# Where the first fp16 part of the attention weights is made, and the model of times behind an engine order

## The chip, the cores and the metric

The kernel runs on one core of a Trainium2 chip. The metric is the device time of one execution in microseconds; the median of several executions counts. A core has five engines that run side by side and meet at semaphores: TensorE (PE in the profile, its weight loads PEld), VectorE (DVE), ScalarE (ACT), GpSimd (POOL), and SyncE (SP), whose queue issues every DMA of this kernel.

## The reference

One decoder layer on x of 512 tokens by 1024 channels, float32, with two attention mixers in parallel:

```python
h = rms_norm(x, norm_w)
proj = h @ w_in                      # q, k, v of both mixers, gates z_a, z_b, gate_b, gate_m
o_a = moba_mixer(...)                # 8 heads of 64
o_b = nsa_mixer(...)                 # 8 heads in 2 groups: compressed, selected and window branch
y_a = o_a * silu(z_a); y_b = o_b * silu(z_b)
g_m = sigmoid(gate_m)
merged = g_m[..., :D] * (y_a @ w_branch_a) + g_m[..., D:] * (y_b @ w_branch_b)
out = x + merged @ w_out
# in each attention unit, for causal keys:
logits = q @ k.T * scale + bias_tab[t5_bucket(dist)]
p = softmax(where(dist >= 0, logits, -1e30)); o = p @ v
```

At 512 tokens every block of the block-sparse mixers is among the selected ones, so the selected and window branches and mixer A are causal softmax attention with a relative bias. There are 24 such units: 8 heads of mixer A, and 8 heads of mixer B with two branches each.

## The kernel before

**Products.** Large products are made in split precision: each float32 operand is a high part (rounded to TensorE's format) and a low remainder, and three matmuls are summed (`mm3`, L418). The high part of a weight tile is made by ScalarE or GpSimd (L386 to L388, L362 to L364), the low part by VectorE or GpSimd as a subtraction (L390, L366). Projections with tokens as rows are `gemm_tok` (PSUM tiles `pgt`), those with channels as rows `gemm_chan` (`pgc`), the branch products `branch` (`pbr`), and the last one `products` (`po`).

**Attention units.** A `Unit` handles one head and branch in four query blocks b of 128, with L = 128 (b + 1) keys. For each block: two matmuls give the scores in PSUM (`sps`, L1044, L1045); VectorE adds the bias, leaves the result in the SBUF tile `sb` and takes the extreme of each row (L1065); ScalarE takes the exponential and its sum (L1076) and multiplies the sum by the gate (L1078); VectorE takes the reciprocal (L1079). P is then kept as two fp16 tiles: GpSimd writes the first part, the exponential times the reciprocal (L1080), and VectorE the remainder (L1081). `send` issues one DMA transpose of both parts (`dma_transpose`, L230) into the tile `dst`, which frees `sb` when it has landed; `pv` multiplies the transposed parts by V (L1094, PSUM tile `O`), and `o_out` (L1121, L1125) takes the result out. There are 6 `sb` buffers, 2 score buffers, 1 `O` and 2 `dst`.

**What sets the order.** The program switches the automatic scheduler off and writes each engine's order by itself. While the program is built, a planner in Python plays the work through: `Chain` objects hold the steps of one piece of work, each step with a dictionary of costs in ns by engine ("A" ScalarE, "D" or "d" VectorE, "P" or "p" GpSimd). `step` gives the step to the engine on which it would end first; the small letters "d" and "P" also mark steps that keep VectorE and GpSimd from working at the same time (`lock`, in `ends`). A step's result is put `OUT[engine] + LAT` ns after its end. Streams of TensorE work (`Run`: scores, values, products, preparation) are generators; the main loop takes the next one that is ready by a margin, and by its share. `dma` and `dma_transpose` issue a transfer on SP at the planner's current time and return when it should have landed; `free["Q"]` is the time at which the transfer engines are free. So every cost in the planner can change the order on all five engines, and the engine of a step with a choice. The chip then runs that fixed order, each engine waiting at its semaphores.

The costs by which a step with a choice is placed:

```python
def cd(n):    return 65 + 1.045 * n
def cg(n):    return 180 + 2.08 * n
def either(n):    return {"d": cd(n), "P": cg(n)}
```

Of the kernel before, what the change touches and what calls it, by code (L numbers as in the profile page):

```python
# [15 lines left out]
AF = mybir.ActivationFunctionType  # L16
ALU = mybir.AluOpType
AX = mybir.AxisListType

S = 512  # L20
D = 1024
DH = 64
P = 128
# [33 lines left out]
MARGIN = 300  # L57
XQ = 1200
XW = 1700.0
# [39 lines left out]
def hybrid_kernel(ctx: ExitStack, tc: tile.TileContext, x, x0, xT, wtok, wchan, gains, w1,  # L99
                  relone, wbr, wout, consts, out):  # L100
    nc = tc.nc
# [18 lines left out]

    now = [0.0]
    heap, seq = [], itertools.count()
    free = {"A": 1900.0, "D": 0.0, "P": 800.0, "Q": 400.0}
    OUT = {"A": 105, "D": 85, "P": 30}
    done = {}
    ap_ = ctx.enter_context(tc.tile_pool(name="att", bufs=NATT))
# [9 lines left out]
    def ca(n):  # L136
        return 93 + 0.834 * n
# [4 lines left out]
    def cd(n):  # L142
        return 65 + 1.045 * n

    def cg(n):
        return 180 + 2.08 * n
# [4 lines left out]
    def either(n):  # L151
        return {"d": cd(n), "P": cg(n)}
# [10 lines left out]
    class Chain:  # L163


        def __init__(c, t=None, held=False):
            c.t = now[0] if t is None else t
            c.q = deque()
            c.held = held
# [49 lines left out]
        def ready(c):  # L219
            return None if c.q else c.t  # L220

    def dma(dst, src, n, t=None):

        nc.sync.dma_start(out=dst, in_=src)
        free["Q"] = max(free["Q"], (now[0] if t is None else t) + 1000) + max(450, n * P / 360)
        return free["Q"] + 1000

    def dma_transpose(dst, src, blocks):

        nc.sync.dma_start_transpose(out=dst, in_=src)  # L230
        free["Q"] = max(free["Q"], now[0] + 1000) + blocks * 120
        return free["Q"] + 1300

    def run_until(t):
        now[0] = max(now[0], t)
# [85 lines left out]
    class Stream:  # L321
# [47 lines left out]
        def split(w, upto):  # L369
            for i in range(w.next, min(upto, len(w.tiles))):  # L370
                w.next = i + 1
                if isinstance(w.tiles[i], Sum):
                    if i not in w.chain:
                        w.split_sum(i)
                    continue
                while i not in w.raw:
                    w.load()
                w.ahead -= 1
                n, *squares = w.tiles[i][1:]
                (raw, t), hi, lo = w.raw.pop(i), w.mk_hi()[:, :n], w.mk_lo()[:, :n]  # L380
                w.out[i] = hi, lo
                c = w.chain[i] = Chain(max(now[0], t))

                def f(e, hi=hi, raw=raw):
                    if e is nc.scalar:
                        e.copy(hi, raw)  # L386
                    else:
                        e.tensor_scalar(hi, raw, 1.0, 1.0, op0=ALU.mult, op1=ALU.mult)  # L388
                c.do({"A": ca(n), "P": 78 + n}, f).mark((w, 0, i))
                c.do(either(n), lambda e, hi=hi, lo=lo, raw=raw: e.tensor_sub(lo, raw, hi.bitcast(F32))).mark((w, 1, i))  # L390
                for o, m, g, acc, fn in squares:
                    c.do({"A": 190 + 0.834 * m}, lambda e, z=raw[:, o:o + m], g=g, acc=acc: e.activation(
                        z, z, AF.Square, scale=g, accum_out=acc)).call(lambda fn=fn, c=c: fn(c.t))
                c.call(w.load)

# [68 lines left out]
    def att(name, dt=F32R):  # L464
        return ap_.tile([P, 512], dt, name=nm(name), tag="a")

    first = alloc("dst", "x0", (P, 2048))
# [348 lines left out]
    def compress_w(kv):  # L816
        st = xws[kv] = []
        b = {}

        def emit(ps):  # L820
            ch = Chain(now[0] + 230)
            for g in range(2):
                for l in range(2):
                    v = lambda z, g=g, l=l: z[g * 64:(g + 1) * 64, :].rearrange("p (j l) -> p l j", l=2)[:, l, :]

                    def f(e, g=g, l=l, v=v):
                        if not g and not l:
                            b["X"] = alloc("gmt", "X", (P, 2, 256))
                        e.tensor_mul(b["X"][64 * l:64 * l + 64, g, :], v(ps), v(R))
                    ch.do({"D": 335}, f, ps if g and l else None, None if g or l else "gmt")  # L830
            for i8 in range(2):
                XW = att("XW", F32).rearrange("p (i g c) -> p i g c", g=2, c=C32)
                ch.do({"p": 140}, lambda e, XW=XW: e.memset(XW[:, :, :, 31:32], 0.0))
                for g in range(2):
                    ch.do(either(248), lambda e, XW=XW, g=g, i8=i8: e.tensor_tensor(
                        XW[:, :, g, 0:31], b["X"][:, g, :].rearrange("p (c i) -> p i c", i=8)[:, :, i8:i8 + 31],
                        pos[:, kv, 8 * i8:8 * i8 + 8].unsqueeze(2).to_broadcast([P, 8, 31]), op=ALU.add),
                        (lambda: b["X"]) if i8 and g else None)
                for q in range(2):
                    xs = att("xs")  # L840
                    split(ch, xs.rearrange("p (i s c) -> p i s c", s=2, c=64),
                          XW[:, 4 * q:4 * q + 4].rearrange("p i g c -> p i (g c)"))
                    st.extend(xs[:, i * P:(i + 1) * P] for i in range(4))
            ch.mark(f"xw{kv}")
        yield from gemm_chan("kc" if not kv else "vc", emit)
# [141 lines left out]
    class Unit:  # L987
# [84 lines left out]
        def soft(u, c, b, z):  # L1072
            L, st = P * (b + 1), u.st
            g = 1.0 / PS if u.gate is None else u.gate[:, b:b + 1]
            s_ = st[:, 2, b:b + 1]
            c.do({"A": 279 + 0.834 * L}, lambda e: e.activation(z["sb"], z["sb"], AF.Exp, bias=st[:, 0, b:b + 1], scale=-1.0,  # L1076
                                                                accum_out=st[:, 1, b:b + 1]))
            c.do({"A": 187}, lambda e: e.activation(s_, st[:, 1, b:b + 1], AF.Copy, scale=g))  # L1078
            c.do({"D": 150}, lambda e: e.reciprocal(s_, s_))  # L1079
            c.do({"P": 315 + 0.834 * L}, lambda e: e.tensor_scalar(z["pp"][:, :L], z["sb"], s_, 1.0, op0=ALU.mult, op1=ALU.mult))  # L1080
            c.do({"d": cd(L)}, lambda e: e.scalar_tensor_tensor(z["pp"][:, L:], z["sb"], s_, z["pp"][:, :L], op0=ALU.mult,  # L1081
                                                                op1=ALU.subtract))
            c.call(lambda: u.send(b, z))
            return c
# [24 lines left out]
    def o_out(O, m, h):  # L1109
        k = (m, h // 2)  # L1110
        row = 64 * (h % 2)
        if row == 0:
            ys[k] = att("ys", F32)
        y = ys[k]
        ch = Chain(now[0] + 230)
        z = {}
        r = vst[:, int(m == "b"), KT + 3:KT + 4]

        def f(e):
            z["t"] = alloc("gmt", "ot", (DH, S))  # L1120
            e.activation(z["t"], O[64:128, :], AF.Copy, scale=r[64:128])  # L1121
        ch.do({"A": 478}, f, None, "gmt")

        def f(e):
            e.scalar_tensor_tensor(y[row:row + 64, :], O[0:64, :], r[0:64], z["t"], op0=ALU.mult, op1=ALU.add)  # L1125
            release(O, ch.t)
        ch.do({"D": 602}, f, lambda: z["t"])
        if row:
            ch.mark(("ys",) + k).call(lambda: y_try(k))
# [422 lines left out]


    class Run:
        def __init__(r, gen, share):
            r.gen, r.share, r.vt, r.wait, r.live = gen, share, 0.0, lambda: 0.0, True

    W.bufs += 1
    for k in range(1, KT):
# [5 lines left out]
    for k in range(KT):  # L1565
# [4 lines left out]
    A, F, C, X, B, V = Run(scores(), SHARE_A), Run(gemms(), SHARE_F), Run(cmp(), SHARE_C), Run(x_rms(), 100.0), Run(prepare(), SHARE_B), Run(  # L1570
        values(), SHARE_V)
# [3 lines left out]
    while any(r.live for r in runs):  # L1575
        live = [r for r in runs if r.live]
        ws = [(r, r.wait()) for r in live]
        ok = ([r for r, w in ws if w is not None and w + MARGIN <= now[0]] or
              [r for r, w in sorted(((r, w) for r, w in ws if w is not None and w <= now[0]), key=lambda z: z[1])[:1]])
        if not ok:  # L1580
            ts = [w for _, w in ws if w is not None] + ([heap[0][0]] if heap else [])
            assert ts, "every stream waits"
            run_until(min(ts))
            continue
        r = min(ok, key=lambda q: q.vt)
        low = min(q.vt for q in ok if q is not r) if len(ok) > 1 else r.vt
        v = next(r.gen, None)
        if v is None:
            r.live = False
        elif callable(v):  # L1590
            r.wait = v
        else:
            r.wait = lambda: 0.0
            r.vt = max(r.vt, low - LAG) + v / r.share
            run_until(now[0] + v)
# [70 lines left out]
```

## Time and profile before

| | |
|---|---|
| median of three runs | 464.18 us (464.04 to 466.37) |
| the profiled execution | 465.96 us, span 464.2 us |
| mean granted TensorE clock | 0.992 |
| busy: PE, DVE, ACT, POOL | 439.8, 374.5, 271.7, 148.2 us |
| instructions: DVE, ACT, POOL | 887, 664, 184 |
| DMA packets, mean rate | 94998, 151 GB/s |

The span runs from the first to the last instruction; the time of an execution includes what lies around it. An engine's busy time holds no waits. A busy share near 100% for PE does not mean that the array runs at its peak, since matmuls overlap. Rows of groups have the form: line, engine, operation, out<-in, shapes, count, then busy time and mean ns of one, then the engine's idle time just before them and what ended it.

### The profile page before, as it was taken

The numbers are of one execution on the slowest core, as the hardware profiler recorded it, in microseconds if no ns is written. First come the engines' busy times: TensorE is split into PE (matmuls) and PEld (weight loads), VectorE is DVE, ScalarE is ACT, GpSimd is POOL, SyncE is SP. The second block draws the span as 40 slices with busy tenths as digits, with TensorE's granted clock in tenths as the row PEclk, the third lists the DMA queues.
The fourth block names the chain that finished last, engine by engine and source line by source line (L and its number), as shares of the span: only waits on it lengthen the run. The fifth ranks groups of instructions, "written<-read, shape, count | busy, mean of one in ns | idle before, by whom it ended". The sixth has DMA issues, their size and how long they took to land.

```text
span 464.2 us, 7259 instructions
## 1 busy us (share of the span) xinstructions
PE 439.8 (95%) x2190; PEld 353.0 (76%) x2190; DVE 374.5 (81%) x887; ACT 271.7 (59%) x664; POOL 148.2 (32%) x184
## 2 busy tenths in 40 slices
PE   9998998898989997999998998979999999999996
PEld 8886887688867776988775775758777887887885
DVE  5757689898988895389987997969894987489993
ACT  7675557676577884366675984746662532352630
POOL 1016125536517552021343442635352320011010
PEclk9999999999999999999999999998999999999999
DMA  8753334669273777320768566277967698442132
GB/s 298 217 153 107 114 114 112 144 124 237 76 225 81 140 191 162 133 68 24 160 148 158 136 147 161 53 153 168 185 153 193 222 335 284 163 160 68 47 136 90
DMA packets 94998, 70.07 MB, mean 151 GB/s; under 512 B 67888, under 2 KB 69808, under 8 KB 94960
## 3 DMA queue, kind: packets, MB, share of 16 engines
q1 hardware_dynamic: 94960, 69.62, 57.0%
q8 instruction: 17, 0.28, 0.2%
q14 instruction: 21, 0.17, 0.1%
HBM read 51.11 MB, written 2.75 MB: 116 GB/s over the span
## 4 chain that ended last, share of the span: by engine, by line
PE 54%; DVE 14%; DMA 12%; ACT 9%; issue 7%; POOL 2%; SPq 1%; DVEq 0%; POOLq 0%; ACTq 0%
PE pgc L418 23%; PE po L418 8%; PE pgt L418 8%; PE pbr L418 6%; DMA dst<-sb 4%; DMA wr<-in_w 3%; DVE wl L390 3%; PE O L1094 3%; DMA wr<-in_wtok 2%; DVE sb L1065 2%; DVE sb L1081 2%; PE sps L1044 2%; POOL sb L1080 2%; ACT sb L1076 1%; ACT wh L386 1%
## 5 line engine op out<-in xcount | busy, mean ns | idle before, releaser
L1080 POOL TENSOR_SCALAR sb<-sb,sst 128x512 f16<-128x512 f32 (+3 forms) x96 | 69.3, 730 | 93.5 <-DVE sst L1079 88.8
L418 PE MATMUL pgc<-hh,wh 128*128 128x512 f32 x208 | 84.0, 404 | 0.1
L390 DVE TENSOR_TENSOR wl<-wr,wh 128x512 fp32r<-128x512 f32 (+1 forms) x99 | 73.4, 757 | 12.6 <-ACT wh L386 10.5
L418 PE MATMUL pgc<-hl,wh 128*128 128x512 f32 x208 | 82.3, 396 | 0.0
L418 PE MATMUL pgc<-hh,wl 128*128 128x512 f32 x208 | 82.2, 395 | 0.0
L1076 ACT ACTIVATE sb<-sb,sst 128x512 f32<-128x512 f32 (+3 forms) x96 | 53.7, 560 | 37.6 <-DVE sst L1065 19.6
L386 ACT CAST wh<-wr 128x512 fp32r<-128x512 f32 (+1 forms) x96 | 58.0, 617 | 12.0 <-DMA wr<-in_wtok 5.3
L1081 DVE SCALAR_TENSOR_TENSOR sb<-sb,sst 128x512 f16<-128x512 f32 (+3 forms) x96 | 57.2, 607 | 2.7 <-POOL sb L1080 2.5
L1065 DVE CUSTOM_DVE_ANT_0 sb<-sps,T 128x512 f32<-128x512 f32 (+3 forms) x96 | 45.4, 481 | 15.3 <-DMA dst<-sb 10.3
L418 PE MATMUL pgt<-wh,hh 128*128 128x512 f32 (+2 forms) x160 | 57.5, 359 | 0.0
L418 PE MATMUL pgt<-wl,hh 128*128 128x512 f32 (+2 forms) x160 | 56.8, 355 | 0.4 <-DVE wl L390 0.4
L418 PE MATMUL pgt<-wh,hl 128*128 128x512 f32 (+2 forms) x160 | 56.6, 354 | 0.0
L418 PEld LDWEIGHTS pgc<-hl,wh 128*128 128x128 f32 x208 | 39.2, 188 | 9.3
L418 PEld LDWEIGHTS pgc<-hh,wl 128*128 128x128 f32 x208 | 39.4, 189 | 7.8 <-DVE wl L390 0.4
L418 PEld LDWEIGHTS pgc<-hh,wh 128*128 128x128 f32 x208 | 39.4, 189 | 7.6 <-ACT s1h L1412 0.5
L1044 PE MATMUL sps<-qs,qs 128*128 128x512 f32 (+2 forms) x80 | 29.6, 372 | 5.7 <-DVE sst L1065 5.6
L418 PEld LDWEIGHTS pgt<-wl,hh 128*128 128x128 f32 x160 | 30.5, 191 | 5.1 <-DVE wl L390 0.9
L418 PEld LDWEIGHTS pgt<-wh,hh 128*128 128x128 f32 x160 | 30.6, 192 | 3.6 <-issue 0.2
L462 POOL TENSOR_TENSOR nr<-nss,mhalf 128x8 f32<-128x8 f32 (+1 forms) x16 | 26.3, 1652 | 21.9 <-DVE nss L461 21.9
L418 PEld LDWEIGHTS pgt<-wh,hl 128*128 128x128 f32 x160 | 30.6, 191 | 3.3
L1045 PE MATMUL sps<-kx,qs 128*128 128x512 f32 (+2 forms) x80 | 26.6, 335 | 0.0
L1094 PE MATMUL O<-dst,vb 128*128 128x512 f16 (+3 forms) x128 | 21.8, 302 | 4.6 <-DMA dst<-sb 4.5
(233 smaller groups left out, 903.3 us busy)
## 6 DMA issues: line engine op xcount, KB each, us to landing
wr<-in_wchan SPq DMA_DIRECT2D x52, 256.0 KB, 3.8
wr<-in_wtok SPq DMA_DIRECT2D x36, 256.0 KB, 3.8
wq<-in_wout SPq DMA_DIRECT2D x36, 256.0 KB, 3.8
T<-rtab SPq DMA_DIRECT2D x16, 256.0 KB, 4.4
wr<-in_w SPq DMA_DIRECT2D x16, 256.0 KB, 2.9
wr<-in_wbr SPq DMA_DIRECT2D x16, 256.0 KB, 3.4
xr<-in_x SPq DMA_DIRECT2D x8, 256.0 KB, 6.0
x<-in_xT SPq DMA_DIRECT2D x7, 256.0 KB, 5.0
```

What stands on the lines that cost most here:

```text
L386: e.copy(hi, raw)
L390: c.do(either(n), lambda e, hi=hi, lo=lo, raw=raw: e.tensor_sub(lo, raw, hi.bitcast(F32))).mark((w, 1, i))
L418: nc.tensor.matmul(dst, sts[i][a], mvs[i][b], start=(start and i == a == b == 0), stop=(stop and i == n - 1 and b == 1), skip_group_check= ...
L462: c.do({"p": 430 + 150 * w}, lambda e: e.tensor_tensor(v(dst), v(ss), mhalf[:parts, :w], op=ALU.pow))
L1044: nc.tensor.matmul(sps[:, :n], qs[:, b * P:(b + 1) * P], ks[:, :n], start=True, stop=False)
L1045: nc.tensor.matmul(sps[:, :n], qs[:, b * P:(b + 1) * P], kx[:, :n], start=False, stop=True)
L1065: e.tensor_tensor_reduce(z["sb"], sps[:, :L], T[:, S - L:], scale=-1.0, scalar=3e38, op0=ALU.add, op1=ALU.min, accum_out=st[:, 0, b:b + 1])
L1076: c.do({"A": 279 + 0.834 * L}, lambda e: e.activation(z["sb"], z["sb"], AF.Exp, bias=st[:, 0, b:b + 1], scale=-1.0, accum_out=st[:, 1, b:b ...
L1080: c.do({"P": 315 + 0.834 * L}, lambda e: e.tensor_scalar(z["pp"][:, :L], z["sb"], s_, 1.0, op0=ALU.mult, op1=ALU.mult))
L1081: c.do({"d": cd(L)}, lambda e: e.scalar_tensor_tensor(z["pp"][:, L:], z["sb"], s_, z["pp"][:, :L], op0=ALU.mult, op1=ALU.subtract))
L1094: nc.tensor.matmul(out, v, u.moving(kb, i), start=(u.first and kb == i == 0), stop=(u.last and kb == 3 and i == 1 and not u.before))
```

## The change

The step that makes the first fp16 part of P gets a choice of ScalarE (an activation with Copy and a scale per partition) or VectorE (`tensor_scalar`) in the place of GpSimd. Beside that, the planner's model of times is altered: the SP queue has a time of its own (`free["S"]`, `issue`), in which a transfer takes 420 ns and a transpose 1230 ns; a transpose then costs 1500 ns, 170 ns per block and 500 ns where it had been 1000, 120 and 1300; the squares of weights, `o_out`, the reciprocal and the addition of positions (`XW`) have new costs. `Run` gets a margin that is the old constant for every stream.

```diff
-    free = {"A": 1900.0, "D": 0.0, "P": 800.0, "Q": 400.0}
+    free = {"A": 1900.0, "D": 0.0, "P": 800.0, "Q": 400.0, "S": 0.0}
...
+    def issue(t, n):
+        free["S"] = max(free["S"], t) + n
+        return free["S"] - n
+
     def dma(dst, src, n, t=None):
 
         nc.sync.dma_start(out=dst, in_=src)
-        free["Q"] = max(free["Q"], (now[0] if t is None else t) + 1000) + max(450, n * P / 360)
+        t = issue(now[0] if t is None else t, 420)
+        free["Q"] = max(free["Q"], t + 1000) + max(450, n * P / 360)
         return free["Q"] + 1000
 
     def dma_transpose(dst, src, blocks):
 
         nc.sync.dma_start_transpose(out=dst, in_=src)
-        free["Q"] = max(free["Q"], now[0] + 1000) + blocks * 120
-        return free["Q"] + 1300
+        free["Q"] = max(free["Q"], issue(now[0], 1230) + 1500) + blocks * 170
+        return free["Q"] + 500
...
-                    c.do({"A": 190 + 0.834 * m}, lambda e, z=raw[:, o:o + m], g=g, acc=acc: e.activation(
+                    c.do({"A": 279 + 0.834 * m}, lambda e, z=raw[:, o:o + m], g=g, acc=acc: e.activation(
...
-                    ch.do(either(248), lambda e, XW=XW, g=g, i8=i8: e.tensor_tensor(
+                    ch.do({"d": 550, "P": 700}, lambda e, XW=XW, g=g, i8=i8: e.tensor_tensor(
...
-            c.do({"D": 150}, lambda e: e.reciprocal(s_, s_))
-            c.do({"P": 315 + 0.834 * L}, lambda e: e.tensor_scalar(z["pp"][:, :L], z["sb"], s_, 1.0, op0=ALU.mult, op1=ALU.mult))
+            c.do({"D": 70}, lambda e: e.reciprocal(s_, s_))
+
+            def first(e):
+                if e is nc.scalar:
+                    e.activation(z["pp"][:, :L], z["sb"], AF.Copy, scale=s_)
+                else:
+                    e.tensor_scalar(z["pp"][:, :L], z["sb"], s_, 1.0, op0=ALU.mult, op1=ALU.mult)
+            c.do({"A": 186 + 0.834 * L, "d": 65 + 0.53 * L}, first)
...
-        ch.do({"A": 478}, f, None, "gmt")
+        ch.do({"A": 571}, f, None, "gmt")
...
-        def __init__(r, gen, share):
+        def __init__(r, gen, share, margin=MARGIN):
...
-        ok = ([r for r, w in ws if w is not None and w + MARGIN <= now[0]] or
+        ok = ([r for r, w in ws if w is not None and w + r.margin <= now[0]] or
```

More of the change, by code (lines that the diff above doesn't have):

```diff
@@ L1554, in hybrid_kernel @@
     class Run:
-        def __init__(r, gen, share):
-            r.gen, r.share, r.vt, r.wait, r.live = gen, share, 0.0, lambda: 0.0, True
+        def __init__(r, gen, share, margin=MARGIN):
+            r.gen, r.share, r.vt, r.wait, r.live, r.margin = gen, share, 0.0, lambda: 0.0, True, margin
     W.bufs += 1
```

## The prediction

> **What bounds the kernel now.** I read the page first: span, busy shares, the chain that ended last.
>
> ```profile
> span 464.2 us, 7259 instructions
> PE 439.8 (95%) x2190; PEld 353.0 (76%) x2190; DVE 374.5 (81%) x887; ACT 271.7 (59%) x664; POOL 148.2 (32%) x184
> PE 54%; DVE 14%; DMA 12%; ACT 9%; issue 7%; POOL 2%; SPq 1%; DVEq 0%; POOLq 0%; ACTq 0%
> ```
>
> TensorE is nearly always busy, so only its idle time (464.2 - 439.8 = 24.4 us), and what a lowered clock costs it, can be won. The chain of waits leaves TensorE for almost half of its length; POOL carries only 2% of it. The second view, busy time by stretch, shows where that half lies.
>
> ```profile
> 40.00:360.00 320.00, 301.70 (x1567) 240.76 (x1566) 266.61 (x700) 202.18 (x532) 130.45 (x158) 0.99 0.58 137
> 360.00:464.20 104.20, 100.42 (x444) 81.28 (x442) 82.36 (x142) 39.43 (x74) 13.29 (x11) 1.00 0.49 167
> ```
>
> The columns are length, then busy PE, PEld, DVE, ACT, POOL, granted clock, DMA share and rate. The attention units run between 40 and 360 us; there PE idles 320 - 301.7 = 18.3 us, DVE is 83% busy, ACT 63%, POOL 41%. After 360 us the kernel is a row of products whose only gap is the output at the end (3.8 us), which the change leaves. So the 18.3 us are the field of play. The third view names their releasers, TensorE's waits (us in total, times, longest):
>
> ```profile
> PE O L1094 <- DMA dst<-sb: 9.7, 7, 2.6
> PE sps L1044 <- DVE sst L1065: 5.6, 8, 1.7
> PE hps L858 <- DVE vl L390: 1.0, 2, 0.6
> PE pgt L418 <- DVE wl L390: 0.4, 1, 0.4
> ```
>
> Half is PV waiting for the transposed P blocks (dst), a third is the score product waiting until DVE has read the PSUM buffer of an earlier score (L1065). The two longest PV waits have a tail. From the order of time, and from the stretches behind them:
>
> ```profile
> 183.19 1.52 PE L1094 MATMUL O<-dst,v 128*128 128x512 f16 x8 [2.63 <-DMA dst<-sb]
> 312.80 1.43 PE L1094 MATMUL O<-dst,vb 128*128 128x512 f16 x8 [2.33 <-DMA dst<-sb]
> 183.20:187.40 4.20, 4.20 (x22) 3.73 (x23) 3.38 (x6) 2.83 (x6) 0.00 (x0) 0.60 0.25 70
> 312.80:317.00 4.20, 4.20 (x17) 3.38 (x18) 4.20 (x14) 3.06 (x10) 2.34 (x4) 0.61 0.66 118
> ```
>
> After each, the granted clock is 0.60 over 4.2 us, with PE fully busy: 0.4 x 4.2 = 1.7 us lost each, 3.4 together.
>
> **The change part by part.** (a) The fp16 part of P (L1080) leaves POOL: 96 pieces, 24 of each length.
>
> ```profile
> L1080 POOL TENSOR_SCALAR sb<-sb,sst 128x512 f16<-128x512 f32 x24 | 23.0, 960 | 40.2 <-DVE sst L1079 40.2
> L1080 POOL TENSOR_SCALAR sb<-sb,sst 128x256 f16<-128x256 f32 x24 | 17.5, 730 | 26.5 <-DVE sst L1079 24.5 <-DVE nss L461 1.9
> L1080 POOL TENSOR_SCALAR sb<-sb,sst 128x384 f16<-128x384 f32 x24 | 16.1, 669 | 15.6 <-DVE sst L1079 13.3 <-issue 1.4 <-DVE nss L461 0.8
> L1080 POOL TENSOR_SCALAR sb<-sb,sst 128x128 f16<-128x128 f32 x24 | 13.3, 561 | 11.1 <-DVE sst L1079 10.8 <-DVE nss L461 0.4
> L885 DVE COPY Gv<-gt 128x512 f32<-128x512 f32 x1 | 0.4, 426 | 0.0
> L877 DVE TENSOR_SCALAR gt<-gt 128x128 f32<-128x128 f32 x2 | 0.4, 216 | 0.0
> L486 ACT ACTIVATE hh<-x,x 128x512 fp32r<-128x512 f32 x7 | 4.9, 727 | 0.4 <-DMA x<-in_xT 0.4
> L392 ACT ACTIVATE wr<-wr,w 128x256 f32<-128x256 f32 x8 | 4.0, 506 | 1.0 <-DVE wl L390 1.0
> ```
>
> POOL: 960 + 730 + 669 + 561 = 2920 ns per unit of four blocks, 730 a piece, 70 us in all. No row shows the piece on DVE; the nearest are one-source operations out of SBUF, 216 ns at 128 columns and 426 at 512, which give 286 and 356 between them: 1284 per unit, 321 a piece, 30.8 us for all. On ACT the nearest are activations with a scale per partition, 506 at 256 and 727 at 512, so 396 and 617 for the others: 2246 per unit, 562 a piece, 53.9 us for all. The planner gives a piece to the engine that ends it first by its own costs; DVE wins unless its queue is over 121 + 0.304 L ns longer than ACT's (0.16 to 0.28 us, from the new costs 186 + 0.834 L and 65 + 0.53 L). DVE being the fuller engine, I take half each (ends: all on one). DVE gains 15.4 us, ACT 27, POOL loses 70. A block's chain shortens by 730 - (321 + 562)/2 = 0.29 us (ends 0.17 and 0.41; below nothing, if DVE or ACT has a queue where POOL had none: POOL's waits above are for the reciprocal, so it stood ready).
>
> (b) What POOL's going gives back to DVE. Subtractions and scalings with all operands in SBUF are longer than those that read PSUM:
>
> ```profile
> L1081 DVE SCALAR_TENSOR_TENSOR sb<-sb,sst 128x512 f16<-128x512 f32 x24 | 21.5, 896 | 2.0 <-POOL sb L1080 1.9
> L1328 DVE SCALAR_TENSOR_TENSOR gm<-gm,pbr 128x512 f32<-128x512 f32 x16 | 10.8, 677 | 3.1 <-PE pbr L418 3.1
> L390 DVE TENSOR_TENSOR wl<-wr,wh 128x512 fp32r<-128x512 f32 x95 | 70.4, 758 | 12.6 <-ACT wh L386 10.5 <-POOL wh L388 1.9
> L1310 DVE TENSOR_TENSOR gm<-pgc,R 128x512 f32<-128x512 f32 x16 | 11.0, 685 | 3.8 <-PE pgc L418 3.8
> 40.00:360.00 320.00, 69.34 (x96) 0.99 0.58 137
> ```
>
> 24 x 0.219 + 95 x 0.073 = 12.2 us of stretching while POOL works. The last row is L1080 alone: 69.34 of POOL's 130.45 us in that stage, 53%. So about 6.5 us come back (ends 0 and 12.2). DVE's net is 15.4 - 6.5 = +9 us: 276 of 320, 86%. ACT goes to 229, 72%; POOL to 61.
>
> (c) The plan of the DMA queue. Every transfer now holds the issuing queue in the model for 0.42 us and every transpose for 1.23, where before neither held it at all. The transposes' own rows:
>
> ```profile
> L230 SPq DMA_TRANSPOSE dst<-sb x96: 1167/1232/2560, 77.2 to 353.1; - x96
> DMA to landing us min/median/max: 2.3/3.0/6.0
> wr<-in_wchan SPq DMA_DIRECT2D x52, 256.0 KB, 3.8
> ```
>
> (min/median/max; for the transfer KB and median us to landing). An issue of 1.23 us is what the model now says. So PV, and the splits of late weights, stand further back in TensorE's order. The order itself is all that this edit touches: no instruction is added.
>
> Its worth is on the seven PV waits, 9.7 us, mean 1.4. One transpose ahead in the queue (1.23) and a chain 0.29 shorter make 1.5, as much as a mean wait; but PV placed later needs other products ready in its place, and holds its sb buffer and O longer. I take half, -4.9 (ends 0 and -9.7). Of the clock tails I take one, -1.7 (ends 0 and -3.4): a 2.63 or 2.33 us wait halved is as short as these two, after which the clock stayed:
>
> ```profile
> 110.13 1.26 PE L1094 MATMUL O<-dst,v 128*128 128x512 f16 x8 [1.45 <-DMA dst<-sb]
> 252.75 0.92 PE L1094 MATMUL O<-dst,vb 128*128 128x512 f16 x4 [1.53 <-DMA dst<-sb]
> 240.00:260.00 20.00, 17.87 (x90) 13.58 (x89) 15.91 (x52) 13.82 (x40) 8.84 (x10) 1.00 0.76 157
> 100.00:120.00 20.00, 18.55 (x134) 17.36 (x133) 17.16 (x45) 12.34 (x34) 11.29 (x9) 1.00 0.85 208
> ```
>
> The Trainium skill (TensorE: Matmul & The Clock Gate, "What's actually happening") puts the fall of the clock after an idle window of about 3.4 us; these waits are shorter and the clock fell, so the measurement decides. By that rule shortening them would not bring the clock back, and the sum would be 1.7 us smaller, 459.3 instead of 457.6.
>
> (d) The score waits, 5.6 us. DVE is 9 us fuller, which lengthens them; but DVE itself waits for sb buffers that a transpose frees:
>
> ```profile
> DVE sb L1065 <- DMA dst<-sb: 10.3, 7, 3.5
> ```
>
> and a shorter chain frees them sooner. I take 0 (ends -3, a third of those 10.3 reaching TensorE, and +4.7, worked out below).
>
> (e) Edits with one answer: the costs of o_out (571), the squares (279), the reciprocal (70) and XW (550 or, on POOL, 700) change the model, not the work; the margin of each stream is the old constant. Freed POOL time draws more low-part subtractions to POOL, at about twice DVE's duration; the splits run ahead of the products, and without that cover the rows L858 and L418 above (1.4 us) grow. Taken as 0, ends -1 and +2.
>
> Sum: -4.9 - 1.7 + 0 + 0 = -6.6 us. The profiled execution took 465.96 us (span 464.2 and 1.8 around it) and would take 459.4; the median of the runs, 464.18, lies 1.8 below it, so 464.18 - 6.6 = 457.6.
>
> **The rivals.** *DVE becomes the bound (slower).* If the planner gives all pieces to DVE, DVE has 266.6 + 30.8 - 6.5 = 290.9 of 320 us, 91%, and its idle time falls from 53.4 to 29.1. Waits that end on DVE (5.6 + 1.4 us) growing in that ratio, 1.83, add 5.8; if the PV waits do not shrink, as the second part of P is behind the same queue, and one more wait passes two microseconds (+1.7), the time is 471.7; with a third of the PV gain, 468. It decides from about 90% of DVE in that stage, or some 87 of the pieces. For it: DVE is already the fullest helper and frees the score PSUM; against it: ACT has 118 us idle there and the planner weighs both.
>
> *The waits only move (no change).* The order's constants (lags, shares, margins) stay while its costs change; PV stands later, and scores, sb buffers or splits are late next. Everything won is waited for elsewhere: 464. For it: the waits listed are many and short, some 0.7 us each on average outside PV; against it: the two long ones cost 8.4 us with their clock and need only be a little shorter.
>
> *The gain is whole.* All PV waits and both tails go, and the sb buffers pull 3 us from the scores: -9.7 - 3.4 - 3 gives 448. Against it: nothing in the plan makes a transpose shorter.
>
> *The port.* DVE pieces stretched by what POOL still runs, for example
>
> ```profile
> L462 POOL TENSOR_TENSOR nr<-nss,mhalf 128x8 f32<-128x8 f32 x12 | 21.4, 1792 | 16.5 <-DVE nss L461 16.5
> ```
>
> With POOL busy 61 of 320 us and half of such a piece to wait, 48 pieces x 0.19 x 0.9 = 8 us more on DVE (89%); score waits and the splits' 1.4 us grow by 53.4/36.4, +3.3: 460.9. The Trainium skill (SBUF — State Buffer, "SBUF: two separate sides") calls the pair of ports that DVE and GpSimd share an exclusive lock, taken also by a DVE operation in a 2-port mode: by that rule moving to DVE keeps part of the quarrel, moving to ACT ends it.
>
> **How the numbers follow.** Forecast 0.42 (own range 453 to 461.5); whole gain 0.10; port 0.10; waits move 0.16; DVE bound 0.22. A tenth or so of each lies over its edge. Under 461.9 (0.5%, about what a measurement here can tell from no change): 0.42 + 0.10 + half of port = 0.57; above 466.5: 0.22 and a little of the moved waits, 0.24; between: 0.19. The range takes in most of the slow and the good case: 450 to 470.
>
> **What would show it.** Right: no POOL row at L1080's successor, about 48 pieces each on DVE (near 320 ns) and ACT (near 560); POOL near 90 us busy in all, ACT near 299, DVE near 383; L1081 at 512 down from 896 to under 800; PV waits under 6 us and at most one stretch at half clock. Wrong: DVE above 90% between 40 and 360 us with longer score waits; PV waits as long as before, or as much idle time with new releasers; or clock tails at new places.

## The result, and the profile after

The changed kernel takes 471.24 us (median of four, 470.75 to 471.69) beside 464.8 for the kernel before: a ratio of 1.0134 (95% interval 1.0101 to 1.0166). Run again later beside its variants it was 1.0103 (1.0070 to 1.0136). It is slower by 5 to 6 us where 457.6 was forecast. The intervals and ratios rest on undisturbed executions alone, the medians on all.

The page of the profile after (the profiled execution took 470.82 us):

```profile
span 468.6 us, 7204 instructions
PE 442.6 (94%) x2190; PEld 354.5 (76%) x2190; DVE 386.4 (82%) x927; ACT 281.0 (60%) x692; POOL 102.4 (22%) x116
PE 50%; DVE 28%; DMA 9%; issue 6%; ACT 5%; POOL 1%; SPq 0%; DVEq 0%; POOLq 0%; ACTq 0%
```

The stretches, with the columns as before (length, PE, PEld, DVE, ACT, POOL, clock, DMA share and rate):

```profile
40.00:360.00 320.00, 299.93 (x1542) 238.35 (x1541) 276.34 (x737) 211.69 (x560) 85.44 (x90) 0.98 0.57 134
360.00:468.60 108.60, 105.29 (x469) 85.55 (x467) 84.30 (x143) 39.49 (x74) 12.38 (x12) 1.00 0.50 169
```

VectorE is at 276.3 of 320 us where 276 was forecast. But TensorE carries out 1542 of its matmuls up to 360 us where it had carried out 1567, so the 4.4 us by which the span is longer were lost ahead of 360 us and show in the tail as the 25 matmuls that are left over. Its waits:

```profile
PE O L1105 <- DMA dst<-sb: 8.3, 4, 3.9
PE sps L1049 <- DVE sst L1070: 7.0, 11, 1.2
PE psv L597 <- ACT nraw L716: 1.7, 1, 1.7
PE O L1105 <- DVE nss L466: 1.1, 1, 1.1
```

The waits of PV for its transposes went from 9.7 to 8.3 us, in four pieces where there had been seven, and the longest is now 3.9 us. That one, seen on three queues in order of time (first column the start, second the duration):

```profile
169.74 0.33 DVE L1092 SCALAR_TENSOR_TENSOR sb<-sb,sst 128x128 f16<-128x128 f32 x1
170.58 5.36 SPq L228 DMA_DIRECT2D wr<-in_wchan  x3
175.99 1.17 SPq L235 DMA_TRANSPOSE dst<-sb  x1
179.18 1.18 PE L1105 MATMUL O<-dst,v 128*128 128x512 f16 x3 [3.92 <-DMA dst<-sb]
179.40:182.70 3.30, 3.30 (x15) 2.53 (x14) 0.74 (x2) 1.32 (x3) 1.36 (x2) 0.50 0.85 268
285.30:291.90 6.60, 6.60 (x23) 5.42 (x23) 3.72 (x12) 0.00 (x0) 0.00 (x0) 0.50 0.66 180
76.97:80.38 3.41, 3.41 (x10) 2.73 (x11) 3.35 (x10) 3.22 (x8) 1.02 (x1) 0.50 0.41 79
```

VectorE had both parts of P ready at 170.07. The transpose was issued at 175.99, since three weight loads stood before it in SyncE's queue and the queue waits in order for the buffers that the loads overwrite (one load waited 3.1 us for ScalarE to be done with its buffer). PV waited 3.92 us, and TensorE's clock was half for the next 3.4 us; a second stretch of low clock, 6.8 us, follows a PV wait of 1.68 us at 284 us, and a third of 3.4 us stands at 77 us. Before there were two, of 3.4 us each. So 6.8 us of array time went to the clock in this execution, and 3.4 before. The pieces of P themselves:

```profile
L1090 DVE TENSOR_SCALAR sb<-sb,sst 128x512 f16<-128x512 f32 x16 | 7.9, 491 | 0.1
L1090 DVE TENSOR_SCALAR sb<-sb,sst 128x128 f16<-128x128 f32 x13 | 3.6, 290 | 0.0
L1088 ACT ACTIVATE sb<-sb,sst 128x512 f16<-128x512 f32 x8 | 5.7, 716 | 1.2 <-DVE sst L1084 1.1
L1088 ACT ACTIVATE sb<-sb,sst 128x128 f16<-128x128 f32 x11 | 4.3, 391 | 0.4 <-DVE sst L1084 0.4
L1092 DVE SCALAR_TENSOR_TENSOR sb<-sb,sst 128x512 f16<-128x512 f32 x24 | 17.8, 743 | 0.1
```

51 of the 96 pieces fell to VectorE and 45 to ScalarE.

### The profile page after: what moved, and what is told of

Read it like the earlier page. It is cut to its first block, busy times and chain, and to the rows that moved or that the text cites. A ratio compares the mean times of both kernels' runs of the same rounds, so it can differ in the third digit from the quotient of the medians.

```text
span 468.6 us, 7204 instructions
## 1 busy us (share of the span) xinstructions
PE 442.6 (94%) x2190; PEld 354.5 (76%) x2190; DVE 386.4 (82%) x927; ACT 281.0 (60%) x692; POOL 102.4 (22%) x116
## 4 chain that ended last, share of the span: by engine, by line
PE 50%; DVE 28%; DMA 9%; issue 6%; ACT 5%; POOL 1%; SPq 0%; DVEq 0%; POOLq 0%; ACTq 0%
PE pgc L423 16%; PE pgt L423 10%; PE po L423 8%; DMA dst<-sb 7%; DVE sb L1092 6%; PE pbr L423 6%; PE pgf L677 5%; DVE sb L1070 5%; DVE wl L395 3%; DVE sb L1090 2%; DMA wr<-in_w 2%; DVE qs L977 2%; ACT sb L1081 2%; PE O L1105 2%; DVE sst L1084 1%
## 5 line engine op out<-in xcount | busy, mean ns | idle before, releaser
L1081 ACT ACTIVATE sb<-sb,sst 128x512 f32<-128x512 f32 (+3 forms) x96 | 53.4, 557 | 28.3 <-DVE sst L1070 27.7
L391 ACT CAST wh<-wr 128x512 fp32r<-128x512 f32 (+1 forms) x84 | 50.5, 614 | 13.5 <-DMA wr<-in_wchan 5.5
L1092 DVE SCALAR_TENSOR_TENSOR sb<-sb,sst 128x512 f16<-128x512 f32 (+3 forms) x96 | 54.4, 583 | 0.3
L393 POOL TENSOR_SCALAR wh<-wr 128x512 fp32r<-128x512 f32 (+1 forms) x24 | 17.2, 720 | 119.4 <-DVE sb L1092 32.3
L467 POOL TENSOR_TENSOR nr<-nss,mhalf 128x8 f32<-128x8 f32 (+1 forms) x16 | 28.3, 1775 | 30.3 <-DVE nss L466 24.3
L395 POOL TENSOR_TENSOR wl<-wr,wh 128x512 fp32r<-128x512 f32 x12 | 16.6, 1384 | 74.4 <-ACT wh L391 34.5
L1088 ACT ACTIVATE sb<-sb,sst 128x384 f16<-128x384 f32 (+3 forms) x45 | 24.3, 547 | 11.1 <-DVE sst L1084 11.0
```

The costliest lines, as they stand in the source:

```text
L467: c.do({"p": 430 + 150 * w}, lambda e: e.tensor_tensor(v(dst), v(ss), mhalf[:parts, :w], op=ALU.pow))
L1088: e.activation(z["pp"][:, :L], z["sb"], AF.Copy, scale=s_)
```

## The experiments

The theories: the fuller VectorE is what costs ("VectorE's time"); the new model of times, by a worse order, is what costs ("the order"); and, from e3 on, the old order was a lucky draw among many ("the draw").

**The old order, the piece elsewhere.** The planner is left in the belief that GpSimd makes the piece, so TensorE's, SyncE's and most other queues keep the order of before; only the engine of the instruction differs.

```diff
-            c.do({"P": 315 + 0.834 * L}, lambda e: e.tensor_scalar(...))
+            c.do({"P": 315 + 0.834 * L}, lambda e: nc.scalar.activation(..., AF.Copy, scale=s_))   # e1
+            c.do({"P": 315 + 0.834 * L}, lambda e: nc.vector.tensor_scalar(...))                     # e2
```

> The order of before on TensorE, VectorE and SyncE, with all 96 pieces of the first fp16 part carried out by ScalarE in place of GpSimd (the planner does not know it). If moving the piece is itself harmful or useful, it shows here without a new order. Theory 'the order': a piece is 0.17 us shorter on ScalarE (562 against 730 ns), the ports are free of 70 us of GpSimd; ScalarE gets 54 us more but has over 100 idle: 460 to 465 us. Theory 'a fuller helper engine is the cause': ScalarE's exponentials and high parts queue behind the pieces: 468 us or more.

> The order of before on TensorE, ScalarE and SyncE, with all 96 pieces carried out by VectorE. Theory 'VectorE is the bound': 96 pieces of about 0.4 us (as in the trace of the changed kernel) put 38 us on it, less what the ports give back, some 290 to 295 us of 320 busy between 40 and 360 us: 470 us or more, with longer waits of the score products. Theory 'the order': 463 to 467, as the piece no longer passes to another engine and back.

On ScalarE: 1.0006 of before (0.9962 to 1.0050), with medians of 467.6 and 465.4 us, between the two forecasts. On VectorE: 1.0219 (1.0150 to 1.0287), 10 us. The stretch and the score waits of e1, then of e2:

```profile
40.00:360.00 320.00, 300.92 (x1555) 239.76 (x1555) 259.46 (x697) 241.65 (x628) 59.74 (x62) 0.98 0.58 134
PE sps L1044 <- DVE sst L1065: 8.1, 10, 1.7
```

```profile
40.00:360.00 320.00, 295.49 (x1523) 231.80 (x1522) 285.36 (x790) 200.65 (x528) 60.04 (x61) 0.99 0.56 130
PE sps L1044 <- DVE sst L1065: 10.5, 13, 1.7
```

With an unchanged order the piece costs nothing that is clear of the noise on ScalarE, which is busy for 242 of the 320 us with it, and is dear on VectorE.

**Load without a chain.** Before, with one more scaling of the same length on VectorE per block that nobody reads (added work):

```diff
+ nc.vector.tensor_scalar(scr[:, :L], cst[:, :L], 1.0, 1.0, op0=ALU.mult, op1=ALU.mult)   # after the GpSimd piece
```

> Before, in its own order, with the piece still on GpSimd; for each of the 96 blocks VectorE does one more scaling of the same length, out of a constant tile into a scratch tile that nobody reads (added work, part of no chain). If VectorE's time itself is what the moved pieces cost, it is as slow as all pieces on VectorE in the old order: 472 to 478 us. If the place in the block's chain or the way the piece waits is what costs, a load beside the chain is much cheaper: 464 to 468.

1.0320 (1.0274 to 1.0365), 14 us: as much as the pieces themselves on VectorE, or more. So in an order that was not made for it, time on VectorE costs by itself, 10 to 15 us for some 36 us added. The score waits of e5:

```profile
40.00:360.00 320.00, 297.63 (x1505) 232.57 (x1504) 284.52 (x781) 198.62 (x523) 131.16 (x153) 0.98 0.56 129
PE sps L1044 <- DVE sst L1065: 12.6, 19, 2.0
```

**Parts of the change.** Only the choice of engine (e3); only the times of SyncE's queue and of a transpose (e4); the whole change with ScalarE as the only choice (e7).

```diff
 # e3: before
-            c.do({"P": 315 + 0.834 * L}, ...)
+            c.do({"A": 186 + 0.834 * L, "d": 65 + 0.53 * L}, first)
 # e4: before with issue(), free["S"] and the new dma() and dma_transpose()
 # e7: after
-            c.do({"A": 186 + 0.834 * L, "d": 65 + 0.53 * L}, first)
+            c.do({"A": 186 + 0.834 * L}, first)
```

> Before, with only the choice of ScalarE or VectorE for the piece (its new costs), every other cost as before. Theory 'the DMA model in the planner costs the time': 461 to 465 us. Theory 'VectorE's load costs it': 469 to 472 as the changed kernel. Theory 'any new order costs, since the old one was a lucky draw': 466 to 470.

> Before, with only the planner's new times of the SyncE queue and of a transpose; the piece stays on GpSimd, no instruction differs, only the order. Theory 'the DMA model costs the time': 469 to 473 us. Theory 'VectorE's load': 463 to 466. Theory 'lucky draw': 466 to 470.

> The changed kernel with ScalarE as the only choice for the piece. VectorE falls to about 260 us of 320 between 40 and 360 us, ScalarE rises to about 240. Theory 'VectorE's time': 462 to 467 us, as fast as before. Theory 'the new model of times': 469 to 472.

e3: 1.0077 (1.0033 to 1.0120). e4: 1.0008 (0.9960 to 1.0057); the new times of the queue alone neither cost nor bring anything, and PV waits as long as in the changed kernel:

```profile
PE O L1099 <- DMA dst<-sb: 8.3, 4, 3.1
PE sps L1049 <- DVE sst L1070: 5.6, 6, 1.6
```

e7: 1.0037 (1.0005 to 1.0070). Up to here most fitted "VectorE's time": the pieces on VectorE seemed to be the loss. But e3 is a new order too, with 40 pieces on VectorE, and it has a PV wait of 4.9 us at 180 us, where the changed kernel has its longest:

```profile
PE O L1100 <- DMA dst<-sb: 9.0, 7, 4.9
```

**The new order, the piece back on GpSimd.** After, with the instruction sent to GpSimd whatever the planner chose.

> The changed kernel's order, with all 96 pieces carried out by GpSimd as before (the planner still believes in ScalarE and VectorE). Takes 51 pieces, some 20 us, off VectorE without a new order. Theory 'VectorE's time': 463 to 467 us. Theory 'the new order': it stays at 469 to 472, or above since the chain of a block is longer than planned.

1.0164 (1.0110 to 1.0219), against "VectorE's time" as I had put it. VectorE is busy only 267 us of the stretch, but it stands still for the piece, which the plan had put elsewhere and shorter:

```profile
40.00:360.00 320.00, 296.73 (x1528) 234.25 (x1527) 267.09 (x683) 191.46 (x514) 151.61 (x185) 0.98 0.56 131
DVE sb L1088 <- POOL sb L1086: 12.6, 19, 1.5
```

So this run does not part the two theories: an order and the engines it was made for belong together.

**Less on VectorE than before.** e7 with the reciprocals on GpSimd, as a power of -1:

```diff
-            c.do({"D": 70}, lambda e: e.reciprocal(s_, s_))
+            c.do({"p": 580}, lambda e: e.tensor_tensor(s_, s_, mone, op=ALU.pow))
```

> As the run with ScalarE alone, and the 96 reciprocals (153 ns each, 14.7 us) go from VectorE to GpSimd as a power of -1, in some 0.7 us each. VectorE at about 245 us of 320. Theory 'VectorE's time' in its plain form (0.5 us of time for each us on VectorE): 457 to 461 us, faster than before. If VectorE ceases to bind below some 265 us, or the block's chain (0.6 us longer) counts: 463 to 468.

1.0023 (0.9992 to 1.0054), VectorE at 261.0 of 320, where 245 was forecast and e7 has 266.4: a small step, and again a new order. Nothing is gained: VectorE waits 15.1 us for sb buffers there, against 6.5 in e7 and 10.3 in the kernel before.

```profile
DVE sb L1072 <- DMA dst<-sb: 15.1, 11, 2.8
```

**Other draws of the same program.** One constant, the planner's latency between engines, moved by a nanosecond or two; on the chip it means nothing.

```diff
-LAT = 60
+LAT = 59      # e9 in before, e10 in after;  e15: 58 and e16: 62, in after;  e13: after unchanged
```

> Before, with the planner's latency between engines 59 ns in place of 60: a change that means nothing on the chip, but the planner's choices fall otherwise and all five orders differ. It shows how much of any difference is the draw of an order. Theory 'VectorE's time decides, orders of equal load are alike': within 2 us of before. Theory 'before is a lucky order': 467 to 470 us.

> The changed kernel with 59 ns in place of 60; 50 pieces on VectorE where it had 51. Theory 'VectorE's time': 469 to 473 us like the changed kernel. Theory 'an unlucky order': anywhere from 464 to 473.

> The changed kernel itself, beside its variants on one chip: its order is the same in every execution, so if the order it got is what costs, it is again 1.2 to 1.5% above before (470 to 473 us) while its neighbours are not. If its first result was a matter of the chip: within 0.5% of before.

> The changed kernel with 58 ns as the latency between engines: a third order of the same family. Theory 'the draw': anywhere between 462 and 472 us, with the last transpose of the eighth head ahead of or behind blocked loads accordingly. Theory 'VectorE's time': 469 to 473.

> The changed kernel with 62 ns: a fourth order of the same family. Theory 'the draw': anywhere between 462 and 472 us. Theory 'VectorE's time': 469 to 473.

e9: 1.0040 (1.0007 to 1.0072). The changed kernel: 1.0103 at 60 (e13), 0.9998 (0.9964 to 1.0031) at 59, 1.0104 (1.0063 to 1.0145) at 58, 1.0107 (1.0061 to 1.0154) at 62. With 50 pieces on VectorE where the changed kernel has 51, e10 is as fast as before. Its stretch and its PV waits, and SyncE's queue at the place shown above:

```profile
40.00:360.00 320.00, 302.77 (x1571) 239.83 (x1570) 280.11 (x742) 214.75 (x565) 87.37 (x91) 0.99 0.58 140
PE O L1105 <- DMA dst<-sb: 3.6, 6, 0.7
170.86 1.17 SPq L235 DMA_TRANSPOSE dst<-sb  x1
173.86 2.06 SPq L228 DMA_DIRECT2D wr<-in_wchan  x3
```

VectorE is at 280 us, fuller than in the changed kernel, and it costs nothing: "VectorE's time" fell here as the cause of the loss. The orders differ in many places. At the one shown above, the transpose stands behind one load and ahead of the next three here, and behind three in the changed kernel and at 62 ns (there the loads take the queue from 169.74 us on for 5.04 us, the transpose follows at 174.83, and PV waits 4.8 us). At 58 ns it also stands behind one load only, and yet that order is slow; its longest wait is another, and whether that one is the cause was not tested:

```profile
254.06 0.69 PE L1049 MATMUL sps<-qs,qs 128*128 128x384 f32 x1 [2.99 <-DVE sst L1070]
```

**That one transpose.** After, with transfer 116 of SyncE's queue issued ahead of 113 to 115; all other queues as in the changed kernel.

```diff
     def dma(dst, src, n, t=None):
-        nc.sync.dma_start(out=dst, in_=src)
+        nq[0] += 1
+        if nq[0] in LATER:                  # (113, 114, 115): kept until the transpose is issued
+            late.append((dst, src))
+        else:
+            nc.sync.dma_start(out=dst, in_=src)
...                                         # in dma_transpose: then issues what was kept
```

> The changed kernel with one exchange on the SyncE queue: the last transpose of the eighth head of mixer A, which stood behind three loads that waited for their buffers until 175.9 us, is issued ahead of them; all other engines keep their orders. Theory 'a transpose behind blocked loads': PV's wait of 3.9 us at 179 us falls under 1 us, one stretch of low clock goes with it, and the time is 3 to 5 us less than the changed kernel's on the same chip. Theory 'VectorE's time': less than 1 us, the wait comes back elsewhere.

1.0041 (1.0013 to 1.0069) where the changed kernel beside it is 1.0103 (1.0070 to 1.0136): 2.9 of its 5.3 us (467.2, 470.1 and 464.8), just under the 3 to 5 forecast and just outside the noise. The PV wait at 179 us is gone; of it 1.8 us comes back as a wait for the next weights of the compression at 182 us. The profiled execution still has three stretches of low clock, so the one did not go there as forecast; over all executions the mean clock is 0.995 against 0.991, some 2 us of array time, so that most of the gain may lie in the clock. The waits:

```profile
PE O L1115 <- DMA dst<-sb: 4.8, 4, 2.1
PE hps L872 <- ACT vh L401: 1.8, 1, 1.8
```

**Versions meant to win.** Fewer pieces on VectorE by a planned cost 200 ns higher, 35 in place of 51 (e11); ScalarE or GpSimd, no VectorE (e12); e11 with its own two late transposes put ahead of the two loads before them (e17); and the same kind of exchange in the kernel before (e18).

```diff
+            c.do({"A": 186 + 0.834 * L, "d": 265 + 0.53 * L}, first)          # e11, e17
+            c.do({"A": 186 + 0.834 * L, "P": 315 + 0.834 * L}, first)         # e12
+    LATER = (113, 114)                     # e17, until transfer 116 is issued
+    LATER = (112, 113, 116, 117, 119)      # e18, until transfers 115, 118 and 120 are issued
```

> The changed kernel with 200 ns more in the planner's cost of a piece on VectorE: 35 pieces there in place of 51, the rest on ScalarE. Theory 'VectorE's time': between the run with ScalarE alone (466) and the changed kernel (471): 467 to 470 us, VectorE near 273 us of 320.

> The changed kernel with the choice of ScalarE or GpSimd for the piece, VectorE excluded (35 on GpSimd). Meant to beat both: ScalarE has 20 us less than alone, VectorE nothing more. Theory 'VectorE's time': 461 to 465 us. If the ports that GpSimd shares with VectorE count, or TensorE's order has nothing left to fill: 465 to 467.

> The kernel with 35 pieces on VectorE, with the last two transposes of the eighth head of mixer A issued ahead of the two loads that held them from about 169 to 174.3 us. Theory 'a transpose behind blocked loads': its PV wait of 4.0 us at 179 us falls under 2 us and the time is 2 to 4 us less than with 35 pieces alone (0.998 of before), so faster than both kernels: 0.990 to 0.994 of before. Rival: the wait moves to the next late release: 0.996 to 1.000.

> The kernel before, with the same kind of exchange for its eighth head: four transposes are issued ahead of the five loads that stood before them between 170.6 and 179.3 us; the piece on GpSimd, all other engines in their old order. Theory 'a transpose behind blocked loads': PV's wait of 2.6 us at 183 us falls under 1 us and the time is 2 to 4 us less: 0.991 to 0.996 of before. Rival: the loads that come later instead delay the splits of the next weights by as much: 0.998 to 1.003.

e11: 0.9979 (0.9942 to 1.0016), as fast as before with VectorE at 278 us, and that with a wait at 179 us as long as the changed kernel's. The profile puts this wait down to VectorE; the exchange of e17 takes it away:

```profile
PE O L1105 <- DVE zs L1310: 4.0, 1, 4.0
```

e12: 1.0038 (1.0003 to 1.0073), no gain. e17: 0.9898 (0.9863 to 0.9932), 461.56 us beside 466.1: faster than both kernels, with VectorE at 280 us.

```profile
span 457.7 us, 7198 instructions
40.00:360.00 320.00, 305.76 (x1592) 242.84 (x1592) 280.13 (x733) 222.88 (x581) 88.50 (x93) 1.00 0.61 143
PE O L1115 <- DMA dst<-sb: 1.1, 1, 1.1
PE sps L1059 <- DVE sst L1080: 9.2, 13, 1.2
```

The PV waits are nearly gone, and in this execution there is no stretch of low clock ahead of the end. The score waits are now the largest in sum, each 1.2 us at most. e18: 0.9996 (0.9964 to 1.0027). Its PV wait of 2.6 us at 183 us is gone as forecast, and the loads that now come later are waited for instead:

```profile
PE O L1104 <- DMA dst<-sb: 6.4, 6, 1.8
PE hps L867 <- ACT vh L396: 1.6, 1, 1.6
```

There the rival was right: the loads were needed as soon as the transposes. The exchange paid in two orders and not in this one; it can pay only where the delayed loads are not waited for as long.

## Why the prediction was wrong

**The load was right, in part by luck.** VectorE in the stretch: 276 forecast, 276.3 measured; ScalarE 229 against 211.7, GpSimd 61 against 85.4, since more low parts and casts went to GpSimd than I had allowed for (my sign for GpSimd over the whole span, near 90, did not follow from my own sum either: 148.2 - 70 = 78; it was 102.4). But VectorE's terms were off and made up for each other. The 51 pieces there took 19.8 us where I had 15.4 for 48 of them: 491 and 290 ns at 512 and 128 columns where I took 426 and 216. The scalar per partition is not what makes them dear, as e5's scalings by plain numbers into fp16 took 515 and 288; what does is not told apart. Of term (b)'s 6.5 us only 2.7 came back on L1081 (57.2 to 54.4 us in the stretch): at 512 columns it fell from 896 to 743 ns, as forecast, but at 256 it rose from 503 to 537. The low parts did not become shorter, 771 ns at 512 columns where they had been 756. The rest of the agreement is work that went to GpSimd or past 360 us.

**Term (c) failed first, -4.9 us.** I took half of the PV waits from the planner's truer times of the queue. They are 8.3 us where they were 9.7, in the changed kernel and with the new times alone (e4), and e4's time is that of before. The new model charges each issue, but not the wait of a load for its buffer, and a transpose behind such a load is held all the same: 5.9 us at 170 us. I had seen SyncE's issue times and not asked what stands before a transpose and what it waits for.

**The clock term failed with it, -1.7.** I had gone by the length of a wait: halved, it would be as short as the two of 1.45 and 1.53 us after which the clock stayed. There was no long wait less but a longer one, and the clock cost 3.4 us more than before in the profiled execution, with one of the three stretches behind a wait of only 1.68 us. The Trainium skill (TensorE: Matmul & The Clock Gate, "What's actually happening") has the clock fall after an idle window of about 3.4 us, and says that the window runs freely. The traces here agree with the free-running window and not with the idle: a window in which TensorE is busy for up to about half of the time was enough (last section). So what counts is how much of one window a wait takes up together with the gaps beside it, and not its length alone. The clock is no full account of the loss either: the second profile of the changed kernel (e13) lost only 2.0 us to it and took 467.4 us.

**Term (d), taken as zero, was +1.4.** The score waits went from 5.6 to 7.0 us. The measured 471.24 lies close to the 471.7 of the rival "DVE becomes the bound", by coincidence: that was for all pieces on VectorE at 91% of the stretch, and here it was 51 of them at 86%. With all 96 in the old order (e2) VectorE was at 89% and the time at 477. And VectorE's load does not set apart fast orders from slow ones: e10, e11 and e17 carry 278 to 280 us at 1.000, 0.998 and 0.990 of before, the orders at 60, 58 and 62 ns 276 to 281 at 1.010.

**What the runs put in their place.** The loss belongs to the order that was drawn. One place in it, a transpose behind three blocked loads, is shown by exchange to hold 2.9 of 5.3 us (e14). It is not by itself what sets the changed kernel behind the old one: before, PV waits 2.6 us at about the same place (183 us), and e11 is as fast as before with a wait of 4.0 us there. The remaining 0.4% is as large as the step between two draws of the kernel before (e9), and is not explained further. Three of four draws of the changed planner are 1% above before, two draws of the old one at 0 and 0.4%: whether the new costs draw worse orders on the whole stays open, four against two are too few. The forecast's fault was not in a price of an instruction but in holding a new order to be the old one with shorter waits. I had listed "the waits only move" with 0.16 and had the slow side rest on VectorE alone; a slow side from the order, as wide as a draw, was missing. Of the signs of being wrong that I had named, two came: PV waits nearly as long as before, and clock tails at new places.

## What to carry to other kernels

Where a planner writes the order, measure first how far the time moves under a change that means nothing (here 1 ns of a planning constant moved it by up to 1%), and hold an edit's gain against that spread, not against the noise of one program. Look in the queue that issues transfers for ones that are ready and stand behind others that wait for a buffer; exchange them where the blocked ones have time, as it gave 0.8% in one order here and nothing in another. And test an engine's load with the plan made for it: 36 us put on VectorE in the old order cost 10 to 15 us, while planned orders with some 14 to 20 us of it took from about 1% more to 1% less than before; the full load in a plan of its own was not tried.

## What the hardware showed that was not expected

**The clock goes by windows of 3.41 us, and half a window of standing still is enough.** In each of the 20 traces the stretches of low clock begin and end on one grid of 3.413 us (in the changed kernel at 76.97, 179.37 and 285.18 us: 30 and 31 windows apart). Three windows of that grid in the changed kernel, with TensorE's busy time first behind the length:

```profile
175.96:179.37 3.41, 0.19 (x1) 0.13 (x2) 1.66 (x4) 1.20 (x6) 1.87 (x2) 1.00 0.77 205
250.99:254.40 3.41, 1.79 (x11) 1.31 (x12) 1.70 (x5) 1.76 (x4) 0.62 (x1) 1.00 0.67 136
281.77:285.18 3.41, 1.73 (x14) 1.26 (x13) 3.31 (x7) 2.59 (x5) 0.00 (x0) 1.00 0.49 94
```

After the first and the third the clock was half; after the second, which holds a PV wait of 1.90 us, it stayed. Over all traces the clock fell 43 times from full: after every one of the 24 windows in which TensorE was busy for less than 44%, after 13 of the 20 with 44 to 54%, and after 6 of the 2584 with more. These 6, one of them at 77 us here, are not explained; the busy time rests on modelled ends of matmuls.

**The scatter of one and the same program goes with that clock.** Over the 114 executions of the kernel before that stand behind the ratios of e1 to e18, the 43 with a mean granted clock of 0.996 or more had a median span of 462.5 us, the 21 below 0.99 (median 0.988) 465.3; the correlation is -0.61. So 2.8 us go with 0.008 of clock, which is 3.7 us of array time; which of the two brings the other along this does not show, since longer waits lower the clock too. The fastest version (e17) also has the highest clock in its profiled execution, 1.000, without a wait of TensorE over 1.4 us.
